# Modulation products of a decoder step: fp32 weights cut into three bf16 parts on the chip

## The chip, the cores and the metric

The kernel runs on one core of a Trainium2 chip. The metric is the device time of one execution in microseconds. Before the change it is 2628.93 us, the median of three runs (2626.52 to 2629.45).

## The reference, cut to what matters

One inference step of a small decoder: layer 0 is a spatial-gating MLP (SGU), layer 1 a sparse attention, and each is followed by a gated MLP with a short convolution (ConvGLU). 1024 prompt tokens and 8 single-token samples go through it, in float32. Every sub-layer is steered by a modulation: shift, scale and gate, six vectors of 1024 for each layer, which come from a condition vector `c` (one for the prompt, eight for the samples):

```python
def ada_params(c, w_ada, b_ada):
    return (jax.nn.silu(c) @ w_ada + b_ada).reshape(c.shape[0], N_MOD, D_MODEL)

def modulate(x, shift, scale):
    return x * (1 + scale[:, None, :]) + shift[:, None, :]
```

So the modulation of a layer is a product of 9 rows of `silu(c)` with a matrix `w_ada` of 1024 x 6144 float32 (25 MB), and there are two layers.

## The kernel before, in words

The framework fixes the order of each engine's instructions when the kernel is built; at run time every engine takes its list in that order and waits on semaphores. Tiles come from pools that hand their buffers out in turn: `raws` (three buffers for what a DMA brings in, float32, 1024 columns), `W` (four for split weights), `T`, `P` and `E` (13, 2 and 2), and two groups of four PSUM banks, `psA` and `psB`.

Most of the work is dense products of a weight piece with the tokens, which lie as columns in chunks of 384, 384 and 264. Each operand is split in two float32r parts: a high part (`whi`, L103 on POOL or the ScalarE) and what is left (`wlo`, `Hl`, `gl`: a subtraction, L106 on POOL or the VectorE), and three products are added up (L84). In the ConvGLU, `gate_part` and `up_part` fill `psA`; the VectorE's L714 convolves, L721 multiplies; the down products fill `psB`, and L634 (for the samples also L637 and L638) adds each finished `psB` bank to the result `R`.

The modulation is computed in three rounds for each layer, 2048 columns of `w_ada` in a round. Round 0 of layer 0 is written apart (`half_step`, L300) and stands at the head of the kernel; its end (`half_end`, `MOD` additions at L314) releases the first affine step. The other five rounds are `ada_round`: a round is 8 steps of 128 rows of `w_ada`, and one last step. A step brings two pieces of 128 x 1024 into buffers (L242, on the DMA queue of SP) and makes four fp32 products (L245): `SCT` (`silu(c)`, 9 columns used of 32) is the weight, 512 columns of `w_ada` are what moves, and each of the four fills its own 32 partitions of one `psB` bank, which the round holds to its end. The last step (`fin`) copies the bank, turns it by four transposes and adds `b_ada` by four additions (L258).

The steps of a round are spread over other work. Those of round 1 go into a queue `fq` and are taken out by `pump` after every second chunk of the SGU's v pieces (80 to 150 us); those of round 2 in the SGU's u pieces (230 to 278 us), two at a time and later one; those of layer 1 stand in `slow` and are taken by `background`, one in four ticks, all through the first ConvGLU (450 to 1057 us).

```python
            if slow and not fq and tick[0] % 4 == 0:
                slow.popleft()()
```

The order that comes out sets a step's four products as one run between dense products, or tears them into two runs. In the order of before the 160 products of the five rounds stand in 63 runs.

Of the kernel before, what the change touches and what calls it, by code (L numbers as in the profile page):

```python
# [17 lines left out]
KT = 8  # L18
# [37 lines left out]
def hybrid_step(  # L56
# [173 lines left out]
            tr(b[:, i * 128:i * 128 + m], PROW[:m, i * 128:(i + 1) * 128])  # L230
        A.activation(PAR, b[:, :NPAR], AF.Copy)

    def ada_round(L, r, mk):

        st = {}

        def step(k):
            if k == 0:
                st["b"] = bank("B")
            rw = [mk(), mk()]  # L240
            for half in range(2):
                SP.dma_start(rw[half][:, :1024],  # L242
                             w_ada[L, k * 128:(k + 1) * 128, 2048 * r + 1024 * half:2048 * r + 1024 * half + 1024])
            for g in range(4):
                PE.matmul(st["b"][32 * g:32 * g + 32, :512], SCT[:, k, :], rw[g // 2][:, (g % 2) * 512:(g % 2 + 1) * 512],  # L245
                          start=(k == 0), stop=(k == KT - 1), skip_group_check=True)

        def fin():
            S = mk()
            A.activation(S[:, :512], st["b"], AF.Copy)  # L250
            b2 = bank("B")
            for j in range(4):
                tr(b2[:, j * 128:(j + 1) * 128], S[:, j * 128:(j + 1) * 128])
            bb = PAR[:, pBADA + L * 48 + 16 * r:pBADA + L * 48 + 16 * r + 16].rearrange("p (g j) -> p g j", j=4)
            mo = MOD[L][:, 16 * r:16 * r + 16, :].rearrange("p (g j) c -> p g j c", j=4)
            src = b2.rearrange("p (j g c) -> p g j c", j=4, g=4)
            for g in range(4):
                V.tensor_tensor(mo[:, g], src[:, g, :, 0:9], bb[:, g].unsqueeze(2).to_broadcast([128, 4, 9]), op=OP.add)  # L258

        out = [lambda k=k: step(k) for k in range(KT)]  # L260
        out.append(fin)
        return out

    def rawmk():
        return raws.tile([128, SLOT], F32, name="raw", tag="raw")
# [278 lines left out]
            half_step(k, aw[1][k], b)  # L544
    half_end(1, b)
    first_affine(1)
    for c in range(3):
        first_h(c, 1)
        for i in range(2):
            z_half(i, c, 1)  # L550
            sgu_v(i, c, zb[i, c])
# [2 lines left out]
    sgu_consts()  # L554
    conv_state(0)
    conv_state(1)
    fq.extend(ada_round(0, 1, lambda: Tt("adaw", tag="P")))
    for i in range(2, 8):
        for c in range(3):
            sgu_v(i, c)  # L560
            if (3 * i + c) % 2:
                pump(1)
        zload(i + 2)
    drain()

# [39 lines left out]
    for i in range(8, 16):  # L605
        m = i - 8
        U[m] = Tt("U", tag="PPTT"[m % 4])
        for c in range(3):
            b = dense(pieces[i], 128, c)
            c0, n = CH[c]  # L610
            A.activation(U[m][:, c0:c0 + n], b[:, :n], AF.Gelu_apprx_tanh, bias=PAR[:, pSBI + m:pSBI + 1 + m])
            pump(2 if i < 12 else 1)
            if i > 11:
                product(m, c)
            if i == 15:
                for k in range(8):
                    split(Hh[:, k, c0:c0 + n], Hl[:, k, c0:c0 + n], VT[k][:, c0:c0 + n], "A", "V")
        if i == 11:
            drain()
            for c in range(3):  # L620
                for k in range(4):
                    product(k, c)
            fq.extend(ada_round(0, 2, rawmk))
        zload(i + 2)
    drain()
    for i in range(18, 24):
# [25 lines left out]
    def conv_glu(l, R, gate, tail_af, last, slow, prefetch=None):  # L652
# [37 lines left out]
        def background():  # L690
            pump(2)
            tick[0] += 1
            if slow and not fq and tick[0] % 4 == 0:
                slow.popleft()()

        for i in range(3):
# [798 lines left out]
```

## Time and profile before

| what | value |
|---|---|
| median of three runs | 2628.93 us |
| profiled execution | 2626.55 us |
| its span | 2624.8 us |
| granted TensorE clock, mean | 0.981 |
| TensorE busy | 2525.8 us, 96% |
| VectorE busy | 1676.1 us, 64% |
| POOL busy | 998.4 us, 38% |
| ScalarE busy | 793.2 us, 30% |

The profiled execution stands 2.4 us under the median. A busy share is an average over stages, and matmuls are pipelined: the duration of a matmul record overlaps that of the next, so what a matmul costs is read from the time between the starts. Idle time of an engine is listed with what ended it; a wait that is listed with "issue" is one for which the trace shows no other engine.

### The profile page before, as it was taken

The numbers are of one execution on the slowest core, as the hardware profiler recorded it, in microseconds if no ns is written. First come the engines' busy times: TensorE is split into PE (matmuls) and PEld (weight loads), VectorE is DVE, ScalarE is ACT, GpSimd is POOL, SyncE is SP. The second block draws the span as 40 slices with busy tenths as digits, with TensorE's granted clock in tenths as the row PEclk, the third lists the DMA queues.
The fourth block names the chain that finished last, engine by engine and source line by source line (L and its number), as shares of the span: only waits on it lengthen the run. The fifth ranks groups of instructions, "written<-read, shape, count | busy, mean of one in ns | idle before, by whom it ended". The sixth has DMA issues, their size and how long they took to land.

```text
span 2624.8 us, 41121 instructions
## 1 busy us (share of the span) xinstructions
PE 2525.8 (96%) x15984; PEld 2369.4 (90%) x15984; DVE 1676.1 (64%) x3913; ACT 793.2 (30%) x1611; POOL 998.4 (38%) x1066
## 2 busy tenths in 40 slices
PE   7999999999999999999999989998999999999996
PEld 5898898999999999998887979777999999999996
DVE  4233346677677767755798987534767677767647
ACT  3121234111111111124576776542311111111121
POOL 3332535233222322335346665534523333222335
PEclk8999999999999999999999989999999999999998
DMA  8314302222222222111114112233211111111111
GB/s 274 124 51 127 105 17 71 91 81 73 89 81 81 89 66 96 60 34 51 60 39 118 42 47 65 69 121 109 65 49 49 49 49 41 41 49 49 49 41 67
DMA packets 203977, 192.15 MB, mean 73 GB/s; under 512 B 9806, under 2 KB 178246, under 8 KB 202999
## 3 DMA queue, kind: packets, MB, share of 16 engines
q1 hardware_dynamic: 200582, 179.86, 21.8%
q0 software_dynamic: 2688, 9.44, 1.1%
q8 instruction: 127, 2.08, 0.3%
q14 instruction: 67, 0.55, 0.1%
q10 hardware_dynamic: 513, 0.23, 0.0%
HBM read 178.41 MB, written 11.27 MB: 72 GB/s over the span
## 4 chain that ended last, share of the span: by engine, by line
PE 80%; DVE 11%; POOL 3%; issue 2%; ACT 2%; DMA 2%; ACTq 0%; SPq 0%; POOLq 0%; DVEq 0%
PE psA L84 50%; PE psB L84 23%; PE psB L185 3%; PE psB L245 2%; DVE Cc L714 2%; DVE junk L948 1%; DVE R L634 1%; PE psA L185 1%; ACT junk L979 1%; DVE S L928 1%; POOL L L1252 0%; DMA raw<-in_dsa_w_out_dram 0%; DMA adaw<-in_w_ada_dram 0%; DVE R L638 0%; PE psA L1308 0%
## 5 line engine op out<-in xcount | busy, mean ns | idle before, releaser
L84 PE MATMUL psA<-Hh,whi 128*128 128x384 f32 (+1 forms) x2896 | 935.6, 324 | 14.7 <-POOL whi L103 7.7
L84 PE MATMUL psA<-Hl,whi 128*128 128x384 f32 (+1 forms) x2896 | 932.4, 322 | 0.1
L84 PE MATMUL psA<-Hh,wlo 128*128 128x384 f32 (+1 forms) x2896 | 929.1, 321 | 0.9 <-DVE wlo L106 0.9
L634 DVE SCALAR_TENSOR_TENSOR R<-psB,g,R 128x384 f32<-128x384 f32 (+1 forms) x952 | 525.6, 568 | 296.0 <-PE psB L84 293.8
L103 POOL TENSOR_SCALAR whi<-raw 128x1024 fp32r<-128x1024 f32 x179 | 194.8, 1089 | 1100.7 <-PE psA L84 962.2
L84 PEld LDWEIGHTS psA<-Hh,whi 128*128 128x128 f32 x2896 | 548.0, 189 | 44.8 <-issue 21.5
L84 PEld LDWEIGHTS psA<-Hl,whi 128*128 128x128 f32 x2896 | 548.6, 189 | 7.2 <-issue 6.1
L84 PEld LDWEIGHTS psA<-Hh,wlo 128*128 128x128 f32 x2896 | 547.9, 189 | 7.6 <-issue 5.0
L106 POOL TENSOR_TENSOR wlo<-raw,whi 128x1024 fp32r<-128x1024 f32 x163 | 403.6, 2476 | 12.7
L84 PE MATMUL psB<-gh,whi 128*128 128x384 f32 (+1 forms) x1056 | 341.9, 324 | 3.4 <-DVE t L637 1.6
L84 PE MATMUL psB<-gl,whi 128*128 128x384 f32 (+1 forms) x1056 | 337.7, 320 | 0.0
L84 PE MATMUL psB<-gh,wlo 128*128 128x384 f32 (+1 forms) x1056 | 337.7, 320 | 0.0
L714 DVE SCALAR_TENSOR_TENSOR Cc<-As,PAR,Cc 128x256 f32<-128x256 f32 (+3 forms) x264 | 262.2, 993 | 56.1 <-ACT Cc L709 54.9
L84 PEld LDWEIGHTS psB<-gh,whi 128*128 128x128 f32 x1056 | 198.4, 188 | 25.6 <-issue 13.8
L84 PEld LDWEIGHTS psB<-gl,whi 128*128 128x128 f32 x1056 | 198.6, 188 | 0.0
L84 PEld LDWEIGHTS psB<-gh,wlo 128*128 128x128 f32 x1056 | 198.5, 188 | 0.0
L101 ACT ACTIVATE gh<-Cc 128x384 fp32r<-128x384 f32 x132 | 64.9, 492 | 437.7 <-DVE Cc L721 437.6
L716 ACT ACTIVATE Cc<-Cc 128x384 f32<-128x384 f32 x132 | 64.9, 492 | 391.2 <-DVE Cc L714 391.2
L708 ACT ACTIVATE As<-psA 128x384 f32<-128x384 f32 x132 | 60.5, 458 | 341.5 <-PE psA L84 341.5
L721 DVE TENSOR_TENSOR Cc<-psA,Cc 128x384 f32<-128x384 f32 x132 | 67.8, 513 | 111.9 <-PE psA L84 111.3
L84 PE MATMUL psB<-Hh,wh 128*128 128x384 f32 (+1 forms) x512 | 137.8, 339 | 1.0 <-POOL wh L103 0.5
L638 DVE TENSOR_TENSOR R<-R,t 128x8 f32<-128x8 f32 x328 | 131.0, 406 | 2.9
(362 smaller groups left out, 3299.6 us busy)
## 6 DMA issues: line engine op xcount, KB each, us to landing
raw<-in_ffn_w_up_dram SPq DMA_DIRECT2D x88, 512.0 KB
raw<-in_w_ada_dram SPq DMA_DIRECT2D x64, 512.0 KB
raw<-in_ffn_w_down_dram SPq DMA_DIRECT2D x44, 512.0 KB
adaw<-in_w_ada_dram SPq DMA_DIRECT2D x32, 512.0 KB
raw<-in_sgu_w_in_dram SPq DMA_DIRECT2D x16, 512.0 KB
raw<-in_dsa_w_in_dram SPq DMA_DIRECT2D x16, 512.0 KB
raw<-in_dsa_w_out_dram SPq DMA_DIRECT2D x32, 256.0 KB
raw<-in_sgu_w_out_dram SPq DMA_DIRECT2D x8, 512.0 KB
```

What stands on the lines that cost most here:

```text
L84: PE.matmul(out, l, r, start=start, stop=stop)
L101: A.activation(hi, src, AF.Copy)
L103: G.tensor_scalar(hi, src, 1.0, 0.0, op0=OP.mult, op1=OP.add)
L106: (V if e_lo == "V" else G).tensor_tensor(lo, src, f(hi), op=OP.subtract)
L185: PE.transpose(out, in_, ident[:in_.shape[0], :in_.shape[0]])
L245: PE.matmul(st["b"][32 * g:32 * g + 32, :512], SCT[:, k, :], rw[g // 2][:, (g % 2) * 512:(g % 2 + 1) * 512], start=(k == 0), stop=(k == KT ...
L634: V.scalar_tensor_tensor(R[c][:, dt, :npr], b[:, :npr], gp[:, dt:dt + 1], R[c][:, dt, :npr], op0=OP.mult, op1=OP.add)
L638: V.tensor_tensor(R[c][:, dt, npr:n], R[c][:, dt, npr:n], t8, op=OP.add)
L708: A.activation(As[:, c0:c0 + n], b[:, :n], AF.Copy)
L714: V.scalar_tensor_tensor(Cc[:, a0:c0 + npr], As[:, a0 - d:c0 + npr - d], w, Cc[:, a0:c0 + npr], op0=OP.mult, op1=OP.add)
L716: A.activation(Cc[:, c0:c0 + n], Cc[:, c0:c0 + n], AF.Gelu_apprx_tanh)
L721: V.tensor_tensor(Cc[:, c0:c0 + n], b[:, :n], Cc[:, c0:c0 + n], op=OP.mult)
```

## The change

In the five rounds of `ada_round` a step becomes two half-steps. Each brings one piece of 128 x 1024 float32 into a `raw` buffer and then takes it apart: `p0` is the upper half of each float32 word, read as bf16 in place by a view with a step of two elements; `x = raw - p0` goes to a tile `adax`; `p1` is the upper half of each word of `x`; `p2 = x - p1` is written as bf16 into the lower halves of `x`. The two subtractions run on the VectorE in the rounds of layer 0 and on POOL in the rounds of layer 1. Then come twelve bf16 products of 256 columns in a row, `p2`, `p1` and `p0` for four column groups each. Their weight `SCB` holds `silu(c)` in three bf16 parts side by side (27 of 32 columns), and is built once by seven small VectorE operations. The last step of a round adds up the three column sets, by 12 additions in place of 4.

The steps are also taken out in other rhythms: after every chunk in the v pieces, two half-steps all through the u pieces, two of five ticks in the background. In round 1 the pieces come into `raw` buffers and no longer into `P` tiles.

```diff
-    def ada_round(L, r, mk):
+    def ada_round(L, r, mk, mkx, eng):
-        def step(k):
-            if k == 0:
+        def step(k, half):
+            if k == 0 and half == 0:
                 st["b"] = bank("B")
-            rw = [mk(), mk()]
-            for half in range(2):
-                SP.dma_start(rw[half][:, :1024],
-                             w_ada[L, k * 128:(k + 1) * 128, 2048 * r + 1024 * half:2048 * r + 1024 * half + 1024])
-            for g in range(4):
-                PE.matmul(st["b"][32 * g:32 * g + 32, :512], SCT[:, k, :], rw[g // 2][:, (g % 2) * 512:(g % 2 + 1) * 512],
-                          start=(k == 0), stop=(k == KT - 1), skip_group_check=True)
+            raw, x = mk(), mkx()
+            c0 = 2048 * r + 1024 * half
+            SP.dma_start(raw[:, :1024], w_ada[L, k * 128:(k + 1) * 128, c0:c0 + 1024])
+            p0 = halves(raw)[0]
+            p1, p2 = halves(x)
+            eng.tensor_tensor(x[:, :1024], raw[:, :1024], p0, op=OP.subtract)
+            eng.tensor_tensor(p2, x[:, :1024], p1, op=OP.subtract)
+            for i, p in enumerate((p2, p1, p0)):
+                for g in range(4):
+                    PE.matmul(st["b"][32 * g:32 * g + 32, 256 * half:256 * half + 256], SCB[:, k, :], p[:, 256 * g:256 * g + 256],
+                              start=(k == 0 and half == 0 and i == 0), stop=(k == KT - 1 and i == 2), skip_group_check=True)
...
+    V.tensor_copy(SCB, parts)
...
-    fq.extend(ada_round(0, 1, lambda: Tt("adaw", tag="P")))
+    fq.extend(ada_round(0, 1, rawmk, lambda: Tt("adax", tag="P"), V))
...
-            fq.extend(ada_round(0, 2, rawmk))
+            fq.extend(ada_round(0, 2, rawmk, lambda: Tt("adax", tag="E"), V))
...
-            if slow and not fq and tick[0] % 4 == 0:
+            if slow and not fq and 2 * tick[0] % 5 < 2:
...
-    slow = deque(x for r in range(3) for x in ada_round(1, r, rawmk))
+    slow = deque(x for r in range(3) for x in ada_round(1, r, rawmk, lambda: Tt("adax"), G))
```

Three places show how the order moves. The first is the TensorE in the first ConvGLU, before: one step of a layer-1 round, torn into a run of one product and one of three between dense products (`gh` and `gl` are the gated activations, `Hh` and `Hl` the tokens).

```order
L84 MATMUL psA<-Hh,wlo 128x384
L245 MATMUL psB<-raw,SCT 32x512
L84 MATMUL psB<-gh,whi 128x384
L84 MATMUL psB<-gl,whi 128x384
L84 MATMUL psB<-gh,wlo 128x384
L245 MATMUL psB<-raw,SCT 32x512 x3
L84 MATMUL psA<-Hh,whi 128x384
```

The same engine and stage after, at a half-step that is torn into runs of two, one and nine pairs of weight load and product.

```order
L84 MATMUL psB<-gh,wlo 128x384
L256 LDWEIGHTS SCB
L256 MATMUL psB<-adax,SCB 32x256
L256 LDWEIGHTS SCB
L256 MATMUL psB<-adax,SCB 32x256
L84 MATMUL psB<-gh,whi 128x384
L84 MATMUL psB<-gl,whi 128x384
L84 MATMUL psB<-gh,wlo 128x384
L256 LDWEIGHTS SCB
L256 MATMUL psB<-adax,SCB 32x256
L84 MATMUL psB<-gh,whi 128x384
```

Over the five rounds the 960 new products stand in 105 runs. The second place is POOL at the start of the first ConvGLU, before: the last splits of the tokens' rest `Hl`, then weights.

```order
L377 TENSOR_TENSOR Hl<-ht,Hh 128x264 x6
L103 TENSOR_SCALAR whi<-raw 128x1024
L106 TENSOR_TENSOR wlo<-raw,whi 128x1024
L377 TENSOR_TENSOR Hl<-ht,Hh 128x264 x2
L103 TENSOR_SCALAR whi<-raw 128x1024
```

After, there:

```order
L252 TENSOR_TENSOR adax<-raw 128x1024
L389 TENSOR_TENSOR Hl<-ht,Hh 128x264 x2
L253 TENSOR_TENSOR adax<-adax 128x1024
L389 TENSOR_TENSOR Hl<-ht,Hh 128x264 x5
L103 TENSOR_SCALAR whi<-raw 128x1024
L389 TENSOR_TENSOR Hl<-ht,Hh 128x264
L106 TENSOR_TENSOR wlo<-raw,whi 128x1024
```

The two subtractions of the first half-step now stand ahead of and between the splits of `Hl`; the other half-steps follow in the same way between the weights. The third place is the VectorE at the head of the kernel, before: from the page index to the first affine factors (`af`).

```order
L840 TENSOR_SCALAR pidx<-pidx,iop 128x8
L314 TENSOR_TENSOR MOD_101<-psB,PAR 128x2x9 x4
L444 COPY af_268<-MOD_101 128x4
L446 COPY af_270<-MOD_101 128x32
L443 TENSOR_SCALAR af_267<-MOD_101 128x4
```

After, there:

```order
L861 TENSOR_SCALAR pidx<-pidx,iop 128x8
L252 TENSOR_TENSOR adax<-raw 128x1024
L568 COPY SCB<-parts 128x256
L253 TENSOR_TENSOR adax<-adax 128x1024
L326 TENSOR_TENSOR MOD_101<-psB,PAR 128x2x9 x4
L456 COPY af_268<-MOD_101 128x4
```

The first half-step's subtractions and the copy into `SCB` now stand ahead of the `MOD` additions.

## Rows read from the trace of the kernel before

**Rows 1.** The page: TensorE's busy time, and the chain of work by line.
```profile
PE 2525.8 (96%) x15984; PEld 2369.4 (90%) x15984; DVE 1676.1 (64%) x3913; ACT 793.2 (30%) x1611; POOL 998.4 (38%) x1066
PE psA L84 50%; PE psB L84 23%; PE psB L185 3%; PE psB L245 2%; DVE Cc L714 2%; DVE junk L948 1%; DVE R L634 1%; PE psA L185 1%; ACT junk L979 1%; DVE S L928 1%; POOL L L1252 0%; DMA raw<-in_dsa_w_out_dram 0%; DMA adaw<-in_w_ada_dram 0%; DVE R L638 0%; PE psA L1308 0%
```

**Rows 2.** Stages: length, busy us of each engine (instructions), granted clock, DMA share, GB/s.
```profile
80.00:160.00 80.00, 80.00 (x508) 70.45 (x507) 5.49 (x14) 10.46 (x19) 22.32 (x13) 1.00 0.45 140
225.00:280.00 55.00, 55.00 (x306) 39.48 (x305) 5.87 (x12) 7.04 (x13) 11.71 (x8) 1.00 0.57 181
435.00:440.00 5.00, 3.69 (x21) 2.67 (x20) 4.82 (x7) 1.35 (x4) 4.47 (x3) 1.00 0.33 98
450.00:1070.00 620.00, 618.41 (x3837) 578.64 (x3836) 435.74 (x910) 103.11 (x223) 177.21 (x102) 1.00 0.26 83
```

**Rows 3.** Line L245 by form: records, duration min/median/max in ns, first and last start.
```profile
L245 PE MATMUL psB<-raw,SCT x256: 589/593/617, 230.9 to 1057.4; 128*32 128x512 f32 x128
```

**Rows 4.** Timeline of PE about a run of four products: start, duration, what.
```profile
85.97 0.34 PE L84 MATMUL psA<-Hh,whi 128*128 128x384 f32 x1
...
86.32 0.33 PE L84 MATMUL psA<-Hh,wlo 128*128 128x384 f32 x1
86.58 1.06 PE L245 MATMUL psB<-adaw,SCT 128*32 128x512 f32 x8
87.58 0.39 PE L84 MATMUL psA<-Hh,wlo 128*128 128x264 f32 x1
87.81 0.28 PE L84 MATMUL psA<-Hh,whi 128*128 128x264 f32 x1
87.93 0.28 PE L84 MATMUL psA<-Hl,whi 128*128 128x264 f32 x1
```

**Rows 5.** Timeline of PE at a run of a single product (two records).
```profile
492.31 1.04 PE L245 MATMUL psB<-raw,SCT 128*32 128x512 f32 x2
493.29 0.44 PE L84 MATMUL psB<-gh,whi 128*128 128x384 f32 x1
```

**Rows 6.** Chain of work at the head of the kernel: start, us, what.
```profile
49.71 0.57 PE psB L300 x8
...
51.93 1.00 PE psB L300 x16
...
54.58 1.04 PE psB L300 x16
...
56.56 0.43 DVE MOD L314 x4
```

**Rows 7.** Lines L106, L638 and L714 by form on DVE, the last two 480 to 1080 us.
```profile
L106 DVE TENSOR_TENSOR gl<-Cc,gh x132: 420/553/2603, 414.8 to 2550.6; 128x384 fp32r<-128x384 f32 x88, 128x264 fp32r<-128x264 f32 x44
L106 DVE TENSOR_TENSOR wlo<-raw,whi x18: 1206/1225/1372, 35.5 to 1822.4; 128x1024 fp32r<-128x1024 f32 x18
L638 DVE TENSOR_TENSOR R<-R,t x128: 151/168/2425, 502.5 to 1066.2; 128x8 f32<-128x8 f32 x128
L714 DVE SCALAR_TENSOR_TENSOR Cc<-As,PAR,Cc x99: 470/610/2589, 482.1 to 1077.0; 128x384 f32<-128x384 f32 x34, 128x256 f32<-128x256 f32 x33, 128x383 f32<-128x383 f32 x16, 128x382 f32<-128x382 f32 x16
```

**Rows 8.** Waits of PE's weight loads, 160 to 300 us: total, times, longest.
```profile
PEld psA L84 <- POOL whi L103: 5.5, 1, 5.5
```

**Rows 9.** Timeline of POOL before 300 us.
```profile
288.80 8.51 POOL L106 TENSOR_TENSOR wlo<-raw,whi 128x1024 fp32r<-128x1024 f32 x1
```

**Rows 10.** Groups by line, 480 to 1080 us, POOL and DVE: busy us, mean ns, idle before.
```profile
L106 POOL TENSOR_TENSOR wlo<-raw,whi 128x1024 fp32r<-128x1024 f32 x49 | 118.6, 2421 | 4.1
L714 DVE SCALAR_TENSOR_TENSOR Cc<-As,PAR,Cc 128x384 f32<-128x384 f32 (+2 forms) x99 | 91.0, 919 | 7.9 <-ACT Cc L709 7.5
L638 DVE TENSOR_TENSOR R<-R,t 128x8 f32<-128x8 f32 x128 | 50.7, 398 | 2.4
L106 DVE TENSOR_TENSOR gl<-Cc,gh 128x384 fp32r<-128x384 f32 (+1 forms) x48 | 49.2, 1024 | 5.0 <-ACT gh L101 4.5
```

**Rows 11.** Waits of PE, 441 to 1060 us: total, times, longest.
```profile
PE psB L84 <- DVE t L637: 1.2, 2, 0.9
```

More of the change, by code (lines that the diff above doesn't have):

```diff
@@ L231, in turn_params, with halves @@
         A.activation(PAR, b[:, :NPAR], AF.Copy)
-    def ada_round(L, r, mk):
+    def halves(t):
+        v = t.bitcast(BF)[:, 0:2048].rearrange("p (c h) -> p h c", h=2)
+        return v[:, 1], v[:, 0]
+    def ada_round(L, r, mk, mkx, eng):
         st = {}
-        def step(k):
-            if k == 0:
+        def step(k, half):
+            if k == 0 and half == 0:
                 st["b"] = bank("B")
-            rw = [mk(), mk()]
-            for half in range(2):
-                SP.dma_start(rw[half][:, :1024],
-                             w_ada[L, k * 128:(k + 1) * 128, 2048 * r + 1024 * half:2048 * r + 1024 * half + 1024])
-            for g in range(4):
-                PE.matmul(st["b"][32 * g:32 * g + 32, :512], SCT[:, k, :], rw[g // 2][:, (g % 2) * 512:(g % 2 + 1) * 512],
-                          start=(k == 0), stop=(k == KT - 1), skip_group_check=True)
+            raw, x = mk(), mkx()
[9 more added lines that the diff above has]
+                              start=(k == 0 and half == 0 and i == 0), stop=(k == KT - 1 and i == 2), skip_group_check=True)
         def fin():
@@ L253, in fin @@
                 tr(b2[:, j * 128:(j + 1) * 128], S[:, j * 128:(j + 1) * 128])
[L254 to L262, printed above, removed]
+            bb = PAR[:, pBADA + L * 48 + 16 * r:pBADA + L * 48 + 16 * r + 16].unsqueeze(2).to_broadcast([128, 16, 9])
+            bb = bb.rearrange("p (h g j) c -> p h j g c", h=2, g=4)
+            mo = MOD[L][:, 16 * r:16 * r + 16, :].rearrange("p (h g j) c -> p h j g c", h=2, g=4)
+            src = b2.rearrange("p (h j g c) -> p h j g c", h=2, j=2, g=4)
+            for h in range(2):
+                for j in range(2):
+                    for i in reversed(range(3)):
+                        V.tensor_tensor(mo[:, h, j], src[:, h, j, :, 9 * i:9 * i + 9], bb[:, h, j] if i == 2 else mo[:, h, j], op=OP.add)
+        return [lambda k=k, h=h: step(k, h) for k in range(KT) for h in range(2)] + [fin]
     def rawmk():
@@ L546, in hybrid_step @@
     first_affine(1)
+    parts = sm.tile([128, KT, 32], BF, name="parts", tag="ht", bufs=2)
+    rest = sm.tile([128, KT, 9], F32, name="rest", tag="x2")
+    V.memset(parts, 0.0)
+    V.tensor_copy(parts[:, :, 0:9], SCT[:, :, 0:9])
+    V.tensor_tensor(rest, SCT[:, :, 0:9], parts[:, :, 0:9], op=OP.subtract)
+    V.tensor_copy(parts[:, :, 9:18], rest)
+    V.tensor_tensor(parts[:, :, 18:27], rest, parts[:, :, 9:18], op=OP.subtract)
+    SCB = sm.tile([128, KT, 32], BF, name="SCB", tag="x1")
+    V.tensor_copy(SCB, parts)
     for c in range(3):
@@ L560, in hybrid_step @@
             sgu_v(i, c)
-            if (3 * i + c) % 2:
-                pump(1)
+            pump(1)
         zload(i + 2)
@@ L611, in hybrid_step @@
             A.activation(U[m][:, c0:c0 + n], b[:, :n], AF.Gelu_apprx_tanh, bias=PAR[:, pSBI + m:pSBI + 1 + m])
-            pump(2 if i < 12 else 1)
+            pump(2)
             if i > 11:
```

## The prediction

> **What bounds the kernel now.** I read the page's busy shares and the chain of work first, then a table by stage, then the lines that the change touches. TensorE is the bound: 2525.8 of 2624.8 us busy, and its dense lines make most of the chain [rows 1]. In the stages that hold the changed rounds it is fuller still: 80.00 of 80 us, 55.00 of 55 us and 618.41 of 620 us, while the VectorE is nearly idle in the first two (5.49 and 5.87 us) and 70% busy in the third (435.74 of 620) [rows 2]. Two short places differ: the start of the first ConvGLU at 435 to 440 us, where DVE is full and PE is not [rows 2], and the wait for a split weight before 300 us [rows 8]. So PE time taken out of the full stages should come off the end, unless DVE or POOL takes over as what is late.
>
> **What is removed.** The five rounds have 40 k-steps of four fp32 products, two records each, at some 0.59 us in the layer-1 rounds [rows 3]. These durations overlap, so the cost is read from start times. In one run of four products (x8 records) the dense matmul before starts at 86.32, the run at 86.58, the next dense matmul at 87.58 and the one after at 87.81 [rows 4]. Of dense matmuls of 384 columns two steps lie between 85.97 and 86.32, 0.175 us each, and those of 264 start every 0.12 us [rows 4]; so the run costs 1.00 us inside, 0.26 − 0.175 = 0.085 at its entry and 0.23 − 0.12 = 0.11 at its exit. A run of a single product (x2 records) takes 493.29 − 492.31 = 0.98 us [rows 5], as long as one of four: the four column groups run side by side, and a k-step that the order tears in two is paid twice. With 0.085 and 0.105 around it a run is 1.18 us on the mean. In the order of before the 160 products of L245 stand in 63 runs (9, 15 and 39 for the two rounds of layer 0 and the three of layer 1): 63 x 1.18 = **74.3 us**.
>
> **What PE gets instead.** 80 half-steps of 12 bf16 products of 256 columns. The order of after has them in 105 runs (15, 15, 75); counting in each run how often its most frequent column group comes gives 259 passes, three for a whole half-step. The fixed part of a run comes from round 0, which already uses 256 columns: a step alone takes 0.57 us and two in a row 1.00 us [rows 6], so a step more costs 0.43 us, two passes of 0.215, and 0.57 − 0.43 = 0.14 us is fixed. With 0.085 and 0.105 that makes 0.33 us for a run. An fp32 pass of 256 columns at 0.215 us is two cycles a column at the granted 2.4 GHz (PEclk 1.00 [rows 2]); I take one cycle for bf16, 0.107 us, as the f32r rows nearly have (264 columns in 0.12, which would be 0.117 for 256 [rows 4]). So 105 x 0.33 + 259 x 0.107 = 34.7 + 27.7 = **62.4 us, 11.9 us less** (9.3 at 0.117). Three things in it aren't in the trace: the bf16 rate, the stride of two elements, and four such streams at once. Below, the bound is no gain on a run (a fixed part larger by 0.11 us eats 11.6); above, a fixed part without the two edge terms, 105 x 0.19 = 20 us better, which I hold unlikely because every run in the trace has them.
>
> **Subtractions on DVE (rounds of layer 0).** 32 half-steps of two at 128x1024, 1.225 us by the same shape on DVE [rows 7]: 78 us, 39 us beside each round. The sgu_v stage has 74 idle DVE us in 80, the u stage 49 in 55 [rows 2]. In the u stage a chunk is 4.2 us of dense work (24 x 0.175) and two half-steps of 0.65, against four subtractions of 1.225, so 5.5 us of PE cover 4.9 us of DVE: hidden, but only just, and each raw buffer is held some 2.5 us longer in a ring of three. At the end of that stage the last subtractions stand among the splits of Hl. There PE already waits 5.5 us for a weight [rows 8], because a subtraction of POOL took 8.51 us while DVE ran its burst [rows 9], against 2.42 elsewhere [rows 10]; six more DVE operations could add 7 us. Most of them come before the last dense piece, so I take 1 us (0 to 7).
>
> **The head of the kernel.** Seven small operations build SCB in DVE's idle time before 56 us. But the copy into SCB has to wait for the last product of round 0, and behind it in DVE's order stand one subtraction of 1.2 us and only then the MOD additions that start at 56.56 us [rows 6], for which the affine step, the ACT and PE wait. Between PE's last product (54.58 + 1.04) and 56.56 there are some 0.9 us [rows 6]; the copy and the subtraction need 1.4: about 0.5 late, and I take 1 us (0 to 3, the upper end if that subtraction's own transfer, issued behind the others on SP, lands after 56 us). The end of a round grows from 4 to 12 additions of 0.2 us, on DVE, and who needs them comes much later: nothing.
>
> **Subtractions on POOL (rounds of layer 1).** 48 half-steps add 96 operations of the form that POOL has as wlo, 118.6 us for 49, 2.42 each [rows 10]: 232 us on an engine that is 177 of 620 busy [rows 2], in front of the weight splits on the same queue. The trace shows what such an operation does to DVE: L638 takes 0.168 us by its median and 50.7 us for 128; L714 0.610 and 91.0 for 99; L106 0.553 and 49.2 for 48 [rows 7, 10]. The excess is 29.2 + 30.6 + 22.7 = 82.5 us over 49 POOL operations, 1.68 us for each. The Trainium skill ("SBUF — State Buffer", section "SBUF: two separate sides") says that a DVE operation with two SBUF inputs and a GpSimd operation exclude each other for a whole instruction; the trace agrees (L638 grows to 2.43 us at most, one POOL operation long [rows 7]), and it speaks against this part of the change. By the rows, 96 x 1.68 = 161 us more bring DVE to 597 of 620 us, 96%. What that costs PE is the largest unknown. Before, 49 such holds cost PE 1.2 us of waiting for psB [rows 11], 0.025 each; 96 at that rate are 2.4 us, which I take, since DVE stays under full. The ends are 0 and the overflow worked out under the second rival. At the stage's start a POOL subtraction goes ahead of the last Hl splits, where DVE and PE are already short [rows 2]: 1 us (0 to 5, its two operations in full).
>
> **Transfers** carry the same bytes, one 512 KB piece for each half-step as before; the raw ring (three) and its slots just turn over with a later release. No term.
>
> **The sum.** −11.9 + 1 + 1 + 2.4 + 1 = −6.5 us. The profiled execution took 2626.55 us (span 2624.8), so 2620.0; it lies 2.4 below the median of 2628.93, so the median comes to **2622.4 us**, 0.25% faster. 0.2%, 5.3 us, is about what a measurement can tell from no change.
>
> **Rivals.** (a) *Every cover holds and the edges shrink*: only 2 us are lost and a run's fixed part is 0.28: −17.2 + 2 = −15, 2613.7. For it: DVE's idle time in layer 0; against it: nothing in the rows shows a cheaper edge. (b) *DVE becomes the bound of the first ConvGLU* (slower). One mechanism: POOL's subtractions hold DVE off, so L634 empties psB late and PE waits for banks. It decides from (620 − 435.74) / 96 = 1.92 us a hold. Two POOL operations that follow each other leave DVE less to do in between than the single ones of before; at 2.2 us a hold DVE needs 647 us and PE loses 27: −11.9 + 4 + 27 = +19, 2648; whole holds of 2.42 give 668 us and +40, 2669. Bursts alone, under full, cost some 15 us: +6, 2635. For it: 1.68 is near 1.92; against it: PE's 1.2 us so far. (c) *Strided bf16 streams don't run at one column a cycle*: at the fp32 pass's 0.215 us the passes cost 27.7 more: +21, 2650. (d) *Products of the four groups don't overlap*, so that twelve in a row are twelve passes: 960 x 0.107 instead of 259 x 0.107, 75 us more: +68, 2697. The trace speaks against it: one run moves 4 x 512 columns twice in 0.98 us [rows 5], as fast as a quarter of that. The Trainium skill ("SBUF — State Buffer", section "A bandwidth-pool intuition that's wrong (but worth ruling out)") gives PE's moving operand one bf16 column a cycle, some 614 GB/s, by which four streams would take turns, as in (d); the fp32 run moves 2.1 MB in 0.98 us, over three times as much, so the trace disagrees. (e) *Buffers late*: the longer hold of the raw ring costs PE some 6 us in all: no change, 2628.
>
> **How the numbers follow.** Forecast 0.42 (2616 to 2628; 0.26 of it faster, 0.16 same), (a) 0.16, (b) 0.25 (0.22 slower, 0.03 same), (c) 0.08, (d) 0.04, (e) 0.05 (same 0.03, slower 0.02). Faster 0.42, same 0.22, slower 0.36. Both signs are likely: the forecast's own range is 2616 to 2628. The range reaches over (a) and over (b) and (c) as worked out with partly full holds, 2611 to 2652, and leaves out (d), the whole holds and a tail of (a), some 0.13.
>
> **What would show it.** PE's runs: a 12-product run at 0.65 us from entry to exit, not 0.97 or 1.5; records of the four groups a few ns apart. In 450 to 1060 us: DVE near 96%, PE over 99% busy, waits of PE for L634 or L638 under 5 us (b shows as tens of us there). POOL's L252 and L253 at 2.4 us each. At 56.5 us: MOD additions less than 1.5 us later. Before 300 us: PE's wait for whi not over 7 us. The prediction is wrong if PE's passes take longer than 0.12 us, or if DVE runs without a gap in the first ConvGLU.

## The result, and the profile after

The changed kernel is slower: 2645.70 us median (2641.18 to 2646.72) against 2627.72 before (the median of four executions by then), a ratio of 1.0069 with a 95% interval of 1.0049 to 1.0089, some 18 us. Its profiled execution took 2641.18 us, 14.6 more than that of before. It is the quickest of its four, so the traces can account for 14.6 of the 18 us and no more.

The page of after, first its busy times, then the chain by line. TensorE's busy time fell by 6.3 us while its span grew by 14.7, so it waits 21 us more; VectorE and POOL have 167 and 189 us more work than in [rows 1] and the table of before.

```profile
span 2639.5 us, 42610 instructions
PE 2519.5 (95%) x16624; PEld 2386.9 (90%) x16624; DVE 1843.2 (70%) x4023; ACT 792.7 (30%) x1611; POOL 1187.3 (45%) x1162
PE psA L84 47%; PE psB L84 23%; PE psB L185 3%; PE psB L256 1%; DVE Cc L735 1%; ACT junk L1000 1%; DVE R L655 1%; DVE R L659 1%; DVE junk L969 1%; DMA raw<-in_dsa_w_out_dram 1%; PE psA L185 1%; DVE S L949 1%; DMA raw<-in_w_ada_dram 1%; POOL whi L103 1%; DVE ht L384 1%
```

The products themselves did what was forecast. The timeline of PE at one half-step, in the form of [rows 4]: the run begins 0.27 us after the dense product ahead of it, the next dense product 0.45 us later, the one after that 0.29 later. By the starts, the 54 runs of twelve cost 0.653 us at the median, entry and exit with it, where 0.651 was worked out.

```profile
99.88 0.34 PE L84 MATMUL psA<-Hl,whi 128*128 128x384 f32 x1
100.15 0.41 PE L256 MATMUL psB<-adax,SCB 128*32 128x256 bf16 x8
100.39 0.28 PE L256 MATMUL psB<-raw,SCB 128*32 128x256 bf16 x4
100.60 0.45 PE L84 MATMUL psA<-Hh,wlo 128*128 128x384 f32 x1
100.89 0.34 PE L84 MATMUL psA<-Hh,whi 128*128 128x384 f32 x1
```

The stages of [rows 2] after (length, busy us of PE, PEld, DVE, ACT, POOL, then the granted clock): PE now idles 4 us of 55 in the u stage, and 7.7 of 620 in the first ConvGLU, where it idled 1.6.

```profile
80.00:160.00 80.00, 79.77 (x639) 73.21 (x638) 53.70 (x59) 10.48 (x19) 23.43 (x14) 1.00 0.51 154
225.00:280.00 55.00, 50.95 (x402) 45.55 (x402) 43.91 (x43) 7.58 (x14) 10.37 (x6) 0.93 0.51 163
450.00:1070.00 620.00, 612.29 (x4120) 584.81 (x4119) 502.68 (x921) 103.79 (x225) 336.13 (x182) 1.00 0.25 78
```

To see where the time went, the dense products (L84) serve as milestones: both traces have 14212 of them, and the time at which the n-th starts is compared. In us against before, positive is later:

| dense product | 800th | 1200th | 1600th | 6800th | 10000th | 14000th |
|---|---|---|---|---|---|---|
| time in before | 194 | 271 | 354 | 1260 | 1930 | 2563 |
| after | +1.2 | −4.6 | +5.7 | +9.7 | +16.4 | +14.5 |

The table tells four things. The head and round (0,1) cost 1.2 us. Round (0,2) gains 5.8 us up to 271 us, and then 10.3 us are lost within 83 us (1.1 of them are work: behind the 1200th product after has seven half-steps left, some 4.6 us, and before three steps, some 3.5). Layer 1's rounds, which end before the 6800th product, cost 4.0 where a saving was expected. And the attention, between the 6800th and the 10000th product, loses 6.7 us, though no instruction of the change is there.

Each trace holds one execution. The 25 executions of the kernel before that one series of runs has beside it reach from 2623.24 to 2638.25 us, and the two kernels `before_tick1` and `before_tick2` (below), whose work is that of before up to 354 us, are already 1.1 and 1.3 us ahead of it at the 800th product. A difference of a microsecond or two in such a table can be chance.

**The end of round (0,2).** The timeline of SP after: the transfers of `sgu_w_out`, which in the kernel before began to leave the queue at 275.0 us, begin at 291.8. First the line of before (up to 290 us), then those of after.

```profile
275.01 9.28 SPq L112 DMA_DIRECT2D raw<-in_sgu_w_out_dram  x4
```

```profile
270.31 13.82 SPq L249 DMA_DIRECT2D raw<-in_w_ada_dram  x4
291.81 18.02 SPq L112 DMA_DIRECT2D raw<-in_sgu_w_out_dram  x6
```

The timeline of POOL after (start, us, what, idle before and what ended it): it stands for 19.6 us until the first of those weights has landed.

```profile
296.07 2.07 POOL L103 TENSOR_SCALAR whi<-raw 128x1024 fp32r<-128x1024 f32 x1 [19.57 <-DMA raw<-in_sgu_w_out_dram]
```

The timeline of DVE after: the last second subtraction, L253, which TensorE needs before it can release the raw buffer, comes at 293.8 us behind a burst of `Hl`.

```profile
290.42 1.96 DVE L106 TENSOR_TENSOR Hl<-V,Hh 128x384 fp32r<-128x384 f32 x4
...
292.75 1.13 DVE L106 TENSOR_TENSOR Hl<-V,Hh 128x264 fp32r<-128x264 f32 x3
293.78 1.30 DVE L253 TENSOR_TENSOR adax<-adax 128x1024 bf16<-128x1024 f32 x1
```

PE's waits after from 255 to 312 us (total, times, longest) are then for the subtractions and for weights.

```profile
PE psB L256 <- DVE adax L253: 4.1, 3, 3.4
PE psA L84 <- POOL wlo L106: 2.7, 2, 1.5
PE psA L84 <- POOL whi L103: 2.5, 2, 1.8
```

The stages after, in ten us each, show that the granted clock (the third number from the right) falls with it: 0.79, 0.86, 0.82 and 0.67 from 270 us on, so between the levels of 1.2 and 2.4 GHz, where before it was 1.00 up to 290 us and 0.85 and 0.81 behind. The first line is that of before from 290 to 300 us, where its PE waits too; the other four are after.

```profile
290.00:300.00 10.00, 4.81 (x27) 4.49 (x26) 7.65 (x16) 2.60 (x8) 10.00 (x4) 0.85 0.17 50
```

```profile
270.00:280.00 10.00, 6.75 (x50) 5.92 (x39) 6.93 (x7) 2.06 (x4) 3.42 (x2) 0.79 0.64 211
280.00:290.00 10.00, 10.00 (x72) 9.03 (x71) 10.00 (x17) 7.30 (x17) 0.00 (x0) 0.86 0.16 52
290.00:300.00 10.00, 4.42 (x41) 2.86 (x39) 9.84 (x25) 3.53 (x10) 3.85 (x2) 0.82 0.45 126
300.00:310.00 10.00, 9.30 (x38) 9.30 (x39) 3.38 (x14) 0.00 (x0) 8.00 (x6) 0.67 0.47 134
```

**Layer 1.** POOL's subtractions are shorter than the rows of before made them: groups by line after, 480 to 1080 us, 2.07 and 1.97 us, not 2.42 [rows 10].

```profile
L253 POOL TENSOR_TENSOR adax<-adax 128x1024 bf16<-128x1024 f32 x38 | 74.6, 1969 | 1.2
L252 POOL TENSOR_TENSOR adax<-raw 128x1024 f32<-128x1024 f32 x36 | 74.4, 2072 | 0.4 <-DMA raw<-in_w_ada_dram 0.4
```

PE's waits for psB after, 441 to 1190 us, are 8.7 us, where before they were 1.6 in that stretch (first line).

```profile
PE psB L84 <- DVE t L637: 1.6, 3, 0.9
```

```profile
PE psB L84 <- DVE t L658: 3.9, 4, 1.0
PE psB L84 <- DVE R L655: 2.9, 4, 1.3
PE psB L256 <- DVE t L658: 1.4, 1, 1.4
PE psB L84 <- DVE MOD L272: 0.5, 1, 0.5
```

### The profile page after: what moved, and what is told of

Its sections match the earlier page's. It is cut to its first block, busy times and chain, and to the rows that moved or that the text cites. A ratio compares the mean times of both kernels' runs of the same rounds, so it can differ in the third digit from the quotient of the medians.

```text
span 2639.5 us, 42610 instructions
## 1 busy us (share of the span) xinstructions
PE 2519.5 (95%) x16624; PEld 2386.9 (90%) x16624; DVE 1843.2 (70%) x4023; ACT 792.7 (30%) x1611; POOL 1187.3 (45%) x1162
## 4 chain that ended last, share of the span: by engine, by line
PE 75%; DVE 12%; POOL 4%; DMA 3%; ACT 3%; issue 2%; ACTq 0%; SPq 0%; POOLq 0%; DVEq 0%
PE psA L84 47%; PE psB L84 23%; PE psB L185 3%; PE psB L256 1%; DVE Cc L735 1%; ACT junk L1000 1%; DVE R L655 1%; DVE R L659 1%; DVE junk L969 1%; DMA raw<-in_dsa_w_out_dram 1%; PE psA L185 1%; DVE S L949 1%; DMA raw<-in_w_ada_dram 1%; POOL whi L103 1%; DVE ht L384 1%
## 5 line engine op out<-in xcount | busy, mean ns | idle before, releaser
L84 PE MATMUL psA<-Hh,whi 128*128 128x384 f32 (+1 forms) x2896 | 937.7, 325 | 15.8 <-POOL whi L103 5.9
L84 PE MATMUL psA<-Hh,wlo 128*128 128x384 f32 (+1 forms) x2896 | 933.7, 323 | 3.2 <-POOL wlo L106 2.7
L84 PE MATMUL psA<-Hl,whi 128*128 128x384 f32 (+1 forms) x2896 | 935.5, 323 | 0.2
L655 DVE SCALAR_TENSOR_TENSOR R<-psB,g,R 128x384 f32<-128x384 f32 (+1 forms) x952 | 522.7, 567 | 242.9 <-PE psB L84 242.0
L84 PEld LDWEIGHTS psA<-Hh,whi 128*128 128x128 f32 x2896 | 550.6, 190 | 26.6 <-issue 7.9
L84 PEld LDWEIGHTS psA<-Hh,wlo 128*128 128x128 f32 x2896 | 550.4, 190 | 9.0 <-issue 4.0
L84 PEld LDWEIGHTS psA<-Hl,whi 128*128 128x128 f32 x2896 | 551.1, 190 | 4.0 <-issue 2.4
L106 POOL TENSOR_TENSOR wlo<-raw,whi 128x1024 fp32r<-128x1024 f32 x163 | 403.1, 2473 | 11.2
L84 PE MATMUL psB<-gh,whi 128*128 128x384 f32 (+1 forms) x1056 | 344.6, 326 | 8.2 <-DVE t L658 3.9
L84 PE MATMUL psB<-gl,whi 128*128 128x384 f32 (+1 forms) x1056 | 338.4, 320 | 0.0
L84 PE MATMUL psB<-gh,wlo 128*128 128x384 f32 (+1 forms) x1056 | 337.9, 320 | 0.0
L735 DVE SCALAR_TENSOR_TENSOR Cc<-As,PAR,Cc 128x256 f32<-128x256 f32 (+3 forms) x264 | 278.2, 1054 | 46.5 <-ACT Cc L730 45.3
L84 PEld LDWEIGHTS psB<-gh,whi 128*128 128x128 f32 x1056 | 198.6, 188 | 20.1 <-DVE R L655 6.3
L84 PEld LDWEIGHTS psB<-gl,whi 128*128 128x128 f32 x1056 | 198.8, 188 | 0.9 <-issue 0.9
L84 PEld LDWEIGHTS psB<-gh,wlo 128*128 128x128 f32 x1056 | 198.8, 188 | 0.2 <-issue 0.2
L659 DVE TENSOR_TENSOR R<-R,t 128x8 f32<-128x8 f32 x328 | 183.9, 567 | 3.2
L84 PE MATMUL psB<-Hh,wh 128*128 128x384 f32 (+1 forms) x512 | 137.7, 340 | 3.0 <-POOL wh L103 2.1
```

Source lines behind the costliest of these rows:

```text
L84: PE.matmul(out, l, r, start=start, stop=stop)
L106: (V if e_lo == "V" else G).tensor_tensor(lo, src, f(hi), op=OP.subtract)
L655: V.scalar_tensor_tensor(R[c][:, dt, :npr], b[:, :npr], gp[:, dt:dt + 1], R[c][:, dt, :npr], op0=OP.mult, op1=OP.add)
L659: V.tensor_tensor(R[c][:, dt, npr:n], R[c][:, dt, npr:n], t8, op=OP.add)
L735: V.scalar_tensor_tensor(Cc[:, a0:c0 + npr], As[:, a0 - d:c0 + npr - d], w, Cc[:, a0:c0 + npr], op0=OP.mult, op1=OP.add)
```

## The experiments

Three theories were set against each other. **A**: the main loss is the ring of raw buffers at the end of round (0,2). **B**: POOL's subtractions in the first ConvGLU hold DVE off. **C**: the order of the attention came out worse, because the framework orders it anew whenever anything ahead of it moves. For C the lists of instructions give a measure: how many of the last entries of TensorE's list stand exactly as in the kernel before (called products below; some are transposes).

**The two halves of the change alone.** In `l0only` layer 1 is as before, in `l1only` layer 0 is. Where old and new rounds stand together, `SCB` and two small tiles lie in other buffers; what that does alone no run shows. The diff is that of l0only, cut to the line that tells it.

```diff
-    slow = deque(x for r in range(3) for x in ada_round(1, r, rawmk, lambda: Tt("adax"), G))
+    slow = deque(x for r in range(3) for x in ada_old(1, r, rawmk))
```

> Rounds 1 and 2 of layer 0 in the new form, the three rounds of layer 1 as before (fp32 products, one step in four ticks); SCT is kept, so SCB lies in another buffer and its copy does not wait. Theory A (the raw ring at the end of round (0,2) is the main loss): the trace of after falls 10 us behind between the 1200th and the 1300th dense product, so this kernel has it too: about 6 us behind at the end of the SGU and at the end, 2634 us. Theory B (POOL's subtractions hold DVE off in the first ConvGLU): nothing of it is left here, 2626 us or less. Theory C (the order of the attention came out worse): the loss of some 6 us after 1540 us comes and goes with the order, which this kernel has a third of: 2628 or 2640.

> The three rounds of layer 1 in the new form with two half-steps in five ticks, the rounds of layer 0 as before. Theory A: 3 us less PE work, some 6 us of waits in the first ConvGLU and its end: 2631 us. Theory B: most of the loss is here, 2640 us. Theory C: 6 us more or not, with the order of the attention.

`l0only` is 2657.91 us (ratio 1.0106, 1.0077 to 1.0134), `l1only` 2651.85 (1.0089, 1.0061 to 1.0118). Each half alone is slower than both together, so the loss is not a sum of what the halves add. A and B alone can't give this. By the milestones `l0only` is 8.1 us late at the 6800th product and 31.8 at the 10000th; `l1only` 3.2 and 23.2. So 24 and 20 us are lost in the attention.

**The pieces of round (0,2) in T tiles**, so that they don't use the raw ring:

```diff
-            fq.extend(ada_round(0, 2, rawmk, lambda: Tt("adax", tag="E"), V))
+            fq.extend(ada_round(0, 2, lambda: Tt("adaw"), lambda: Tt("adax", tag="E"), V))
```

> As after, but the pieces of round (0,2) go into T tiles, not into the ring of three raw buffers. Theory A: the transfers of the output weights leave SP's queue at about 275 to 280 us again, not at 291.8, and some 10 us come back: 2636 us. Rival (the subtractions delay DVE's own splits of Hl, wherever the pieces lie): PE still waits before 300 us, 2644 us.

2637.79 us (1.0032, 1.0020 to 1.0045), 8 us better than after. At the 1600th product it is 1.4 us ahead of before, not 5.7 behind: the ring is a cause in that stage. The transfers of the output weights stand in SP's queue from 234.9 us on. But 3.4 of its 4.8 us are still lost between the 1200th and the 1600th product, and r02T is the best of its kind. Five other kernels below have the pieces of round (0,2) in T tiles, and they lose 5.0 to 5.6 us there; the four that keep the raw ring (after, l0only, l1nosub, l0only_tick2) lose 9.4 to 10.5. So about half of the loss belongs to the ring, as theory A has it, and about half stays, as its rival has it: PE waits at 288 and 290 us for second subtractions that stand behind splits of `Hl` (the timeline of DVE in r02T), and the granted clock then falls to 0.66.

```profile
286.17 2.08 DVE L106 TENSOR_TENSOR Hl<-V,Hh 128x384 fp32r<-128x384 f32 x5
288.14 1.31 DVE L253 TENSOR_TENSOR adax<-adax 128x1024 bf16<-128x1024 f32 x1
289.32 1.48 DVE L106 TENSOR_TENSOR Hl<-V,Hh 128x264 fp32r<-128x264 f32 x4
290.69 1.31 DVE L253 TENSOR_TENSOR adax<-adax 128x1024 bf16<-128x1024 f32 x1
```

The stage from 290 to 300 us of r02T:

```profile
290.00:300.00 10.00, 7.23 (x42) 6.19 (x38) 7.91 (x10) 3.34 (x7) 9.83 (x5) 0.66 0.19 54
```

**Layer 1 without subtractions.** The products of layer 1 read the upper half three times, and no `adax` tile is taken there (the lines for that are left out):

```diff
...
-            eng.tensor_tensor(x[:, :1024], raw[:, :1024], p0, op=OP.subtract)
-            eng.tensor_tensor(p2, x[:, :1024], p1, op=OP.subtract)
+            if L == 0:
+                eng.tensor_tensor(x[:, :1024], raw[:, :1024], p0, op=OP.subtract)
+                eng.tensor_tensor(p2, x[:, :1024], p1, op=OP.subtract)
+            else:
+                p1 = p2 = p0
```

> As after, but in layer 1 the two subtractions are left out and the upper half of the weights is multiplied three times (so the modulation of layer 1 loses its low parts); products, transfers and rhythm stay. Theory B: the waits that POOL's 96 subtractions cause go, PE's waits for psB in the first ConvGLU fall to about 1 us, 6 us or more come back: 2640 us or less. Theory A: 2 to 4 us come back there. If neither: the loss of the stage is in the products' order.

2641.06 us (1.0044, 1.0029 to 1.0058), 4.6 better than after. Between the 1600th and the 6800th product after loses 3.9 us and this kernel gains 2.1, so it is 6.0 us quicker there. That is not the price of the subtractions by itself, because the order of this kernel's products came out worse: its layer 1 has 90 runs where after has 75, and by the medians of each length of run they take 47.4 us where those of after take 41.7. With these 5.7 us the subtractions cost PE nearer 12 us than 6, by this estimate. The waits of the same stretch (441 to 1190 us) fell from 8.7 to 2.9 us, not to 1 as expected:

```profile
PE psB L84 <- DVE R L658: 2.7, 2, 1.4
PE psB L84 <- DVE t L661: 0.2, 1, 0.2
```

The order alone moves this stage too: with the same work before_tick1 (below) gains 1.0 us in it against before and before_tick2 loses 2.7; r02T, r02T_tick37 and r02T_shift3, which differ in the rhythm only, lose 5.9, 2.8 and 10.8. Between 450 and 1070 us the PE of l1nosub is busy 619.78 of 620 us, and its DVE 421.75 where after has 502.68: the 80 operations that POOL has more in that stretch (182 against 102) lengthen DVE's work by 1.01 us each. So part of B is true: PE does wait, though DVE is only 81% busy.

```profile
450.00:1070.00 620.00, 619.78 (x4158) 588.73 (x4156) 421.75 (x928) 105.85 (x228) 178.09 (x102) 1.00 0.26 78
```

**The kernel before with its steps at another tick.** This is the test of C without the change: the same products, the same tiles, the same bytes.

```diff
-            if slow and not fq and tick[0] % 4 == 0:
+            if slow and not fq and tick[0] % 4 == 2:
```

> The kernel before, with the background steps at tick 2 of four instead of tick 0: the same work and the same products, but the order of the attention comes out otherwise, and only the last 4539 products of TensorE stand as before. Theory C (the order of the attention in the kernel before is a lucky one, and any change ahead of it loses it): slower by 15 to 22 us between 1430 and 1900 us, as l0only and l1only, 2645 us. Theory A (the loss of the changed kernels is in what they add): no difference, 2628 us.

2652.23 us (1.0085, 1.0068 to 1.0101): as slow as the changed kernel or slower, by nothing but an order. At the 6800th product it is 1.4 us late, at the 10000th 26.1. Two of PE's waits grew, one for ACT (L1265), one for splits on DVE (L106). The waits of PE before, 1430 to 1900 us:

```profile
PE psA L84 <- ACT raw L1265: 2.9, 3, 1.6
...
PE psB L84 <- DVE wh L106: 0.4, 1, 0.4
```

The same of before_tick2:

```profile
PE psA L84 <- ACT raw L1265: 8.1, 4, 4.9
PE psB L84 <- DVE wh L106: 6.2, 6, 1.7
```

Tick 1 gives a third order, the one that r02T and l1nosub have.

> The kernel before with the background steps at tick 1 of four: the same work once more, and the order of the attention that r02T and l1nosub have (the last 4545 products of TensorE as before). Theory C: it loses between 1430 and 1900 us what those two lose there, 7 to 10 us, 2638 us. If the order of the attention isn't the cause, 2630 us.

2633.30 us (1.0026, 1.0011 to 1.0042), 7.3 more than the kernel before beside it; it loses 6.6 us in the attention, where r02T loses 6.4 and l1nosub 5.9.

**r02T with the order of before in the attention.** With another rhythm of the background steps the end of TensorE's list agrees with that of before over the whole attention.

```diff
-            if slow and not fq and 2 * tick[0] % 5 < 2:
+            if slow and not fq and 3 * tick[0] % 7 < 3:
```

> r02T with three half-steps in seven ticks instead of two in five. The last 8644 products of TensorE, the attention with them, then stand in the order of the kernel before. Theory C: the 8 us that r02T loses in the attention are gone, 2629 us or a little less. If the loss there is made by something else (tiles, transfers), it stays at 2638 us.

> r02T with the two half-steps at other places of the five ticks; the last 7950 products stand in the order of the kernel before. As the run with three in seven: 2629 us by theory C, 2638 otherwise.

r02T_tick37 loses 1.3 us in the attention, not 6.4, as C says. But at the end it is 2636.68 us (1.0024, 1.0014 to 1.0034), which isn't clear of r02T's ratio of 1.0032, where C wanted 1.000: it is 3.7 us late at the 6800th product, and 2.9 us more come after the 10000th, which no theory here explains. r02T_shift3 speaks against the measure: it shares 7950 products and still loses 7.4 us in the attention, 2646.11 us (1.0057, 1.0040 to 1.0074). The lists of the other engines don't explain it: by the traces its last 1069 ScalarE instructions are those of before, against 1143 in r02T_tick37, but r2only and r2_and_l1 (below) have 1022 and lose 2.7 and 0.8 us. It enters the attention 10.4 us late, later than these three. And 4.0 of its 7.4 us fall between the 9400th and the 9700th dense product (1826 to 1882 us), where every other kernel with the order of before loses as much: r2only 3.5, r2_and_l1 4.3, r02T_tick37 4.0, l0only_tick2 6.1. That the one traced execution of before was lucky there would fit, but is not shown. So a nearly equal order does not make the time of the attention equal to better than some 7 us.

**Subtractions of layer 1 on DVE.**

```diff
-    slow = deque(x for r in range(3) for x in ada_round(1, r, rawmk, lambda: Tt("adax"), G))
+    slow = deque(x for r in range(3) for x in ada_round(1, r, rawmk, lambda: Tt("adax"), V))
```

> r02T with the subtractions of layer 1 on the VectorE instead of POOL. Its attention has the order of l0only (last 4539 products), so the time at the end says little; the stage up to 1190 us does. Theory B (POOL's operations hold DVE off there): 96 operations of 1.3 us on DVE are 125 us and hold nobody, PE's waits for psB fall and the stage is 3 to 5 us shorter than in r02T. Against it: DVE's own queue gets longer, and it is as long or longer. At the end 2650 us.

2675.42 us (1.0169, 1.0152 to 1.0186). The stage is not shorter but 15.4 us longer than in r02T (21.3 lost between the 1600th and the 6800th product, against 5.9). The expectation fell, but not by waits: those of PE for psB, 441 to 1190 us, are 7.4 us, a little under the 8.4 of r02T.

```profile
PE psB L84 <- DVE t L658: 5.2, 9, 1.4
PE psB L84 <- DVE R L659: 2.2, 2, 1.6
```

What grew is the order's part: the products of layer 1 stand in 109 runs instead of 75, and by the medians of each length of run these take 54.3 us instead of 41.7, 12.6 of the 15.4. Which engine is the better place for the subtractions this run can't say. The attention adds 27.7, with an order that agrees for 4539 products.

**Round (0,2) alone, and with layer 1.** Two kernels whose attention has the same order, one that agrees with before for 7705 products; in both, round (0,1) is as before, the pieces of round (0,2) lie in T tiles and `SCB` is built shortly ahead of them. The second has the new layer 1 as well.

```diff
-            if slow and not fq and tick[0] % 4 == 0:
+            if slow and not fq and 2 * tick[0] % 5 < 2:
...
-    slow = deque(x for r in range(3) for x in ada_old(1, r, rawmk))
+    slow = deque(x for r in range(3) for x in ada_round(1, r, rawmk, lambda: Tt("adax"), G))
```

> Of the change only round (0,2): its pieces in T tiles, SCB built shortly before it; round (0,1) and layer 1 as before. The last 7705 products of TensorE, with most of the attention, stand as in the kernel before. Theory C: no loss in the attention; of the 7.5 us that the round's products save about 1 to 5 are left at 354 us (DVE's burst at the round's end takes the rest), and the whole is 2 us faster to 2 slower than before. If the losses of the other kernels belong to the products or their tiles, it is 8 us slower or more.

> As r2only, with the three rounds of layer 1 in the new form too (two half-steps in five ticks, subtractions on POOL). Its attention has the order of r2only, so the difference of the two is what layer 1's change does alone: 3 us less on PE, some 5 us of waits by POOL's subtractions, 2 to 4 us slower than r2only by theories A and C; 10 us or more by theory B.

r2only is 2627.18 us against 2630.66 for the kernel before beside it: a ratio of 0.9985, 0.9974 to 0.9996, the only kernel that beats before, by 3.5 us. It is 8.0 us ahead at the 1200th product and 2.4 at the 1600th. Its profiled execution loses that lead between 1826 and 1882 us and ends 1 us behind, so the 3.5 us rest on the medians. r2_and_l1 is 2637.11 us (1.0028, 1.0017 to 1.0038), 9.9 us more. That is layer 1's part with an order that agrees over most of the attention, more than the 2 to 4 us that the expectation put to A and C, and just under B's 10. In the profiles it makes 6.6 us up to the 6800th product (from 2.6 ahead to 4.0 behind). The first ConvGLU of r2only:

```profile
450.00:1070.00 620.00, 619.59 (x3847) 580.39 (x3847) 435.28 (x912) 103.85 (x224) 177.29 (x102) 1.00 0.27 83
```

Of r2_and_l1:

```profile
450.00:1070.00 620.00, 612.33 (x4119) 584.25 (x4118) 505.12 (x923) 103.09 (x225) 332.35 (x180) 1.00 0.25 77
```

PE's waits of r2_and_l1, 441 to 1190 us:

```profile
PE psB L84 <- DVE t L690: 3.8, 4, 1.0
PE psB L84 <- DVE R L687: 2.8, 4, 1.4
```

PE idles 7.7 us instead of 0.4, most of it for a psB bank that DVE has yet to empty; the runs of the rounds take 41.7 us instead of 46.2, their waits left out. These two make 2.8 of the 6.6 us. Another 0.6 stand ahead of layer 1's rounds, and some 3 in gaps of under 0.3 us between dense products, which sum to 13.7 us between the 1600th and the 6800th product instead of 10.8; what makes those longer no run shows.

**l0only at another tick**, so that its attention comes nearer to that of before:

> l0only with the fp32 steps of layer 1 at tick 2 of four; the last 5154 products of TensorE and two thirds of DVE's list then stand as in the kernel before. Theory C: most of l0only's loss after 1430 us (22 us) goes, 2640 us. Otherwise 2658 us.

2636.56 us (1.0024, 1.0013 to 1.0035): against the kernel before beside it (2630.66) it is 5.9 us slower, where l0only is 30.0, so 24 us are gone by one digit in the rhythm; the attention loses 6.3 us instead of 23.7.

All runs together, the loss in the attention (between the 6800th and the 10000th dense product, against before) beside the number of last TensorE products that stand as in before. Each loss is read from one execution:

| last products as before | kernels and their loss in us |
|---|---|
| 4539 | before_tick2 24.6, l0only 23.7, l1only 20.0, r02T_l1dve 27.7 |
| 4545 | before_tick1 6.6, r02T 6.4, l1nosub 5.9 |
| 4670 | after 6.7 |
| 5154 | l0only_tick2 6.3 |
| 7705 | r2only 2.7, r2_and_l1 0.8 |
| 7950 | r02T_shift3 7.4 |
| 8644 | r02T_tick37 1.3 |

The kernels at 4539 products stand clear of the others: 20 to 28 us by an order, and before_tick2 has nothing else. Above that the measure doesn't sort: from 4545 products on the losses lie between 0.8 and 7.4 us at any number. The 6.7 us of after are among these. before_tick1 shows that an order alone can cost as much; that it is the order in after too is likely and not shown.

## Why the prediction was wrong, point by point

- **The products: right.** Before, the 63 runs take 74.7 us without their waits (74.3 worked out); after, 105 runs take 61.9 (62.4). The parts are a little otherwise: a run with one pass has 0.22 us inside, with two 0.335, with three 0.455, so a pass is 0.117 us, as the f32r rows had it (0.107 was taken), and the fixed part inside 0.10, not 0.14. The three things that the trace of before didn't show, the bf16 rate, the stride and the four streams at once, cost nothing; rivals (c) and (d) are out. The Trainium skill ("SBUF — State Buffer", section "A bandwidth-pool intuition that's wrong (but worth ruling out)") gives some 614 GB/s for PE's moving operand and says nothing there of column groups. Read as the bound of all four streams together, as in rival (d), it is not borne out: four products of 256 columns start within some 10 ns and are through in one pass.
- **The head: right in kind, too small.** The `MOD` additions start at 58.16 us, not 56.56; 1.6 us by the row, 1.2 at the 800th product, 1 taken. It was the upper end's reason: DVE stands until the piece has landed. And it was the upper end's size, 3.1 us, because this execution was done with round 0 1.5 us sooner than that of before: from the start of its last product to the `MOD` additions it takes 4.5 us, and 1.4 in before and in every other kernel with the old head. Below, the last products of round 0, after and before, then DVE after.

```profile
L312 PE MATMUL psB<-adaw,SCT x128: 379/391/636, 11.5 to 53.7; 128*32 128x256 f32 x128
```

```profile
L300 PE MATMUL psB<-adaw,SCT x128: 379/391/636, 11.9 to 55.2; 128*32 128x256 f32 x128
```

```profile
55.70 1.23 DVE L252 TENSOR_TENSOR adax<-raw 128x1024 f32<-128x1024 f32 x1 [3.41 <-DMA raw<-in_w_ada_dram]
56.84 0.22 DVE L568 COPY SCB<-parts 128x256 bf16<-128x256 bf16 x1
56.98 1.29 DVE L253 TENSOR_TENSOR adax<-adax 128x1024 bf16<-128x1024 f32 x1
58.16 0.41 DVE L326 TENSOR_TENSOR MOD<-psB,PAR 128x18 f32<-128x18 f32 x4
```

- **The end of round (0,2): the first step that failed.** "Most of them come before the last dense piece, so I take 1 us (0 to 7)": it was 10.3. And "its slots just turn over with a later release. No term" was wrong: rival (e) had the ring as a case of its own with 0.05, while the row on SP's queue would have shown that the output weights follow in the same ring. Out of the ring, in the six kernels with T tiles, 3.4 to 5.6 us are lost, so some 5 belong to the ring and some 5 to second subtractions behind DVE's burst, which the term did price, at 1 us. The sign that was set for it, PE's wait for `whi` not over 7 us, could not show it: that wait is 2.5 us, and the loss stands as waits for L253 and for late weights.
- **The holds on DVE: mis-sized both ways.** 1.68 us a hold and 96% of DVE were too much (1.01 us, 81%); one reason is that the operations are shorter (1.97 and 2.07 us), and that some fall into time when DVE would wait anyway is likely, not shown. But the price for PE, 2.4 us by the rate of single holds, was too little: the runs of layer 1 take 4.5 us less and the stage still 3.9 more, so PE lost some 8 us, and nearer 12 by the estimate from l1nosub. Rival (b) had the kind of it in its last case, bursts while DVE is not full, at 15 us; its main cases and its test wanted DVE full, and PE waits for banks long before. (Its sums take 4 us for the other terms, where the forecast adds up 3, and the last should be +7 by that.) The trace agrees with the lock of the Trainium skill ("SBUF — State Buffer", section "SBUF: two separate sides"), by which a DVE operation with two SBUF inputs and a GpSimd operation that reads SBUF exclude each other: the mean of L659, which reads two operands from SBUF, rises from 0.398 [rows 10] to 0.740 us, and L655, which takes one input from PSUM, stays (0.570 before, 0.567 after).
- **Layer 1 was little gain to begin with.** Of the 11.9 us only some 4 were to come from layer 1, where the new products stand in 75 runs instead of 39; the sum hid this, because it was made over all five rounds at once. Beside r2only the layer-1 part costs 9.9 us. The last term, 1 us at the start of the first ConvGLU, can't be told from the order: between the 1600th and the 2000th product (354 to 427 us in before) after loses 0.9 us, and before_tick1 and before_tick2 lose 3.9 each.
- **The order elsewhere: not in the prediction at all.** It took the order of everything behind the change as given. Of the 14.5 us between the two profiles 6.7 are there. before_tick2 shows that an order, by itself, is worth 25 us in the attention, nearly four times the forecast gain of 6.5. Neither of the two things that were to make the prediction wrong came: the passes take 0.117 us, and DVE has gaps.

The sum by the milestones: +1.2 at the head and in round (0,1), −5.8 and +10.3 in round (0,2), +4.0 in layer 1's rounds, +6.7 in the attention, −1.9 in the last ConvGLU, 14.5 in all. So the saving on the products is real, and the steps that failed are the price of the late subtractions and of the ring at the end of round (0,2) (1 us and nothing taken, 10.3 lost), the price of the holds for PE (2.4 taken, some 8 lost), and the order behind the change (nothing taken, 6.7 lost). Open are the 1.9, the small gaps in layer 1, whether the 6.7 are the order's in after itself, why r02T_shift3 loses 7.4 us with most of the TensorE order of before, and the 3.4 us by which the medians differ more than the traces.

## What to carry to other kernels

Where a framework orders all engines in one go, a change moves the order of everything behind it; before its time is put down to what it does, the same kernel should be run with a neutral shift of the order, and two versions compared whose lists agree behind the change. Even then they differed by up to 7 us here, so one trace of each is not enough for a loss of that size. An order also tears what the change adds: r02T_l1dve lost 12.6 us to more runs, not to the engine that was to be tested. Make a sum stage by stage: a saving that pays in one stage (round (0,2), torn into 15 runs) can be a loss in another (layer 1). An operation that sits between a buffer's landing and its release costs the ring's next customer, here the weights of the next stage, though its engine had time left over the stage (DVE 43.91 of 55 us busy).

## What the runs showed of the hardware that was not expected

POOL's subtraction takes 2.07 us on the mean when one operand is bf16 at a step of two, and 1.97 when the result is so too, against 2.42 for f32 alone at the same 128x1024 [rows 10]. On DVE it is the other way: 1.39 us at the median with the bf16 result, 1.23 without, which is also what f32 alone takes there [rows 7].

```profile
L253 DVE TENSOR_TENSOR adax<-adax x32: 1287/1389/3597, 57.0 to 293.8; 128x1024 bf16<-128x1024 f32 x32
L252 DVE TENSOR_TENSOR adax<-raw x32: 1199/1226/2834, 55.7 to 288.0; 128x1024 f32<-128x1024 f32 x32
```
